# Gaps of 64 bytes between the x and y tiles of a two-layer encoder trunk

## The chip, the cores and the metric

The kernel runs on one core of a Trainium2 chip. The metric is device time in microseconds of one execution. TensorE (PE) multiplies: a LDWEIGHTS instruction (shown as engine PEld) puts a 128x128 stationary operand into the array, a MATMUL streams the moving operand through it; both operands are read from SBUF, and the load for one matmul runs while the matmul before it streams. DVE is VectorE, ACT is ScalarE, POOL is GpSimd, SP issues most DMAs.

## The reference

Two layers over 256 tokens of width 2048. Each is RMSNorm, a token mixer, a residual add, RMSNorm, a gated MLP with a convolution of width 3, a residual add; a last RMSNorm closes it.

```python
h = x
for layer in range(2):
    hn = rmsnorm(h, norm_mix_g[layer])
    h = h + (mlstm_mixer(hn, ...) if layer == 0 else hgrn_mixer(hn, ...))
    h = h + conv_glu(rmsnorm(h, norm_ffn_g[layer]), ffn_w_up[layer], ...)   # D_FF = 5504
return rmsnorm(h, final_g)
```

All is float32. By far the most work is the products of the activations with the weights (mixer in and out, MLP up and down).

## The kernel before

**Float32 in halves.** Every weight is split into a coarse part `wh` and a rest `wl` (lines 144 and 145, ACT and DVE), every activation tile into a coarse half and a rest that lie side by side in one tile of 512 columns (`split`, line 205: columns 0 to 255 are the coarse part of the 256 tokens, 256 to 511 the rest). A product is the sum of three, coarse by coarse, coarse by rest and rest by coarse, all in the float32r form.

**The stream of weights.** One list of chunks runs through the whole kernel (`stream`, line 149). Raw weights come by DMA into three buffers `raw` of 8192 bytes in each partition; pieces of 1024 columns are split into one of four buffers `wh` and one of four `wl` (4096 bytes each). Each chunk loops over k, the 128-row blocks of the contraction, with the activation tile `x = ch.x(k)`. Two forms of chunk do nearly all the work:

- "fm" (features by tokens; the mixers' q, k and gate inputs and MLP up; lines 197 to 200): for each of two column blocks f of the weights, the weights are stationary and the x tile moves: a matmul of 512 columns with `wh`, then one of 256 columns (the coarse half) with `wl`. So two loads and 768 moving columns make one pair.
- "tm" (tokens by features; v, o, gates, the mixers' outputs and MLP down; lines 187 to 191): a quarter of the x tile (128 columns) is stationary, 512 columns of the weights move; three matmuls of 512 columns for each half of the tokens. The last piece of the last chunk has the same three at lines 176 to 178.

A small first chunk has both forms (lines 189 to 194). Side jobs (mixer heads, transposes, norms) are put between these matmuls by a counter of estimated time (`Side.tick`).

**Where the tiles lie.** A pool puts the tiles of its tags one behind the other, in the order in which a tag is first used, each rounded up to 32 bytes; the pools follow one another. The x tiles (`xt0` to `xt15`, line 232) and y tiles (tags `yt0` to `yt15`, `slot`, line 378) are 2048 bytes each and lie in the pool `keep`, with one buffer each. y tiles hold the mixer's output (`ya`, `yb`) or the MLP's inner activations (`g`). The MLP's inner width is worked in two parts of 22 and 21 blocks; blocks 16 to 21 don't find a place among the sixteen y tiles and lie in the pool `ff` instead (line 379: `where = keep if j < KT else more`). In the built program the byte addresses in a partition are:

| tile | address | modulo 512 |
|---|---|---|
| hx (the residual stream) | 25664 | 64 |
| xt0 ... xt15 | 42048 ... 72768, steps of 2048 | 64 |
| ya0/g0/yb0 ... ya15/g15/yb15 | 74816 ... 105536, steps of 2048 | 64 |
| raw, three | 107584, 115776, 123968 | 64 |
| wh, four | 132160 ... 144448, steps of 4096 | 64 |
| wl, four | 148544 ... 160832, steps of 4096 | 64 |
| g16 ... g21, MLP of layer 0 | 179584 ... 189824, steps of 2048 | 384 |
| g16 ... g21, MLP of layer 1 | 187840 ... 198080, steps of 2048 | 448 |

The slices that a matmul takes start at multiples of 512 bytes in their tiles. Here *distance* means the start of the moving operand less the start of the stationary one, modulo 512. It is 0 for every fm and tm matmul, but for the tm matmuls of MLP down with g16 to g21, where it is 192 in layer 0 (64 - 384) and 128 in layer 1 (64 - 448). Those are 6 or 5 blocks by 2 halves by 3 matmuls, 36 or 30 in each of 16 chunks, 528 in all.

Of the kernel before, what the change touches and what calls it, by code (L numbers as in the profile page):

```python
# [8 lines left out]
F32 = mybir.dt.float32  # L9
F32R = mybir.dt.float32r  # L10
# [5 lines left out]
P = 128  # L16
T = 256
D = 2048
KT = D // P
# [23 lines left out]
RAW = 3  # L43
WB = 4
MIX = 4
FIRST = (0, 1, 2, 4, 7, 10, 13, 16)

LEVELS = (1, 2, 4, 8, 16, 32, 64)
# [4 lines left out]
def trunk_kernel(ctx, tc, xT, x_d, fg_d, pp_d, cst_d, w_first, w_aq, w_ak, w_av, w_ao, w_aout,  # L53
# [4 lines left out]
    keep = ctx.enter_context(tc.tile_pool(name="keep", bufs=1))  # L58
# [9 lines left out]
    hmx = keep.tile([P, 2], F32, name="mhalf")  # L68
    hx = keep.tile([P, KT, T], F32, name="hx")
    hT = [hx[:, k] for k in range(KT)]  # L70
    hm = hx.rearrange("p k t -> p (k t)").rearrange("p (a c) -> p a c", a=2)
    ident = cst[:, C_ID:C_ID + P]

# [45 lines left out]
    def split_weights(chunks):  # L119

        first = True
        for ch in chunks:
            total = ch.nk * ch.width
            cuts = [0]
            if first:
                cuts = [k * ch.width for k in FIRST]
            while cuts[-1] < total:
# [469 lines left out]
    def hgrn(norm, nxt):  # L597
# [24 lines left out]
        def blocks(z, h, a, b):  # L622
            v = z[:, 0:2 * (T + h)].rearrange("k (p x) -> k p x", p=2)[:, :, a:b]
            return v.rearrange("k p (m j) -> k m p j", j=2 * h)[:, :, :, 0:h]
# [32 lines left out]
        def head(hd):  # L657
# [11 lines left out]
            def gather(z, h, tag):  # L669
                m = mp.tile([P, T], F32, tag=tag, bufs=MIX, name=tag)  # L670
                dve.tensor_copy(m.rearrange("k (m p j) -> k m p j", p=2, j=h), blocks(z, h, 0, T))  # L671
                return m
# [229 lines left out]
def build(nc, ins, out_shape=(2, P, D), **kw):  # L902
    ap = {k: nc.dram_tensor("in_" + k, a.shape, mybir.dt.from_np(a.dtype), kind="ExternalInput").ap()
          for k, a in ins.items()}
    out = nc.dram_tensor("out", out_shape, F32, kind="ExternalOutput").ap()
    mscr = nc.dram_tensor("mscr", (64, T), F32, kind="Internal").ap()
    with tile.TileContext(nc, schedule_with_timeline_sim=True) as tc:
        with ExitStack() as ctx:
            trunk_kernel(ctx, tc, ap["xT"], ap["x"], ap["fg"], ap["pp"], ap["cst"], ap["w_first"],
                         ap["w_aq"], ap["w_ak"], ap["w_av"],  # L910
                         ap["w_ao"], ap["w_aout"], ap["w_bq"], ap["w_bv"], ap["w_bg"],
                         ap["w_bout"], ap["w_up"], ap["w_down"], out, mscr, **kw)
# [12 lines left out]
```

## Time and profile before

| | |
|---|---|
| time, median of 3 runs | 2473.65 us (2473.45 to 2473.66) |
| the profiled execution | 2473.85 us |
| its span (first to last instruction) | 2472.1 us |
| granted TensorE clock, mean | 0.999 |
| fm matmuls | 3776 of 512 columns (line 199), 3776 of 256 (line 200) |
| tm matmuls | 3 x 1442 (lines 189 to 191), 3 x 14 (lines 176 to 178) |

Matmuls are pipelined: a 512-column matmul is shown with a duration near 0.39 us though the next starts 0.23 us later. So the speed of PE is read from start to start, or from the number of instructions in a stretch, not from the durations; "busy" for PE means only that something was in flight. A line of the timeline has the start in us, the duration, the engine, the kernel's line and the operation, output<-inputs and their shapes. A line of the windows view has, for a stretch, its length, PE's busy time with the count of its instructions, the granted clock, and the DMA share and rate.

### The profile page before, as it was taken

To read this page: it belongs to the slowest core of one execution; us is meant where nothing else is said; L and a number is where in the kernel's file an instruction comes from. 1 tells how busy PE (TensorE), PEld (TensorE's weight loads), DVE (VectorE), ACT (ScalarE), POOL (GpSimd) and SP (SyncE) were. 2 spreads that over 40 slices of the span, in tenths; PEclk is the share of its full clock that TensorE was granted. 3 is DMA by queue.
4 is the path that set the end of the run, shared out by engine and by line. 5 is a ranking of instruction groups with operands and counts; after the bars stand their busy time and mean duration, and the time that the engine had idled before them with its cause. 6 is when DMAs were issued, how large, how long until landed. Compare 5 with 4: busy or idle time off the path is not lost.

```text
span 2472.1 us, 33659 instructions
## 1 busy us (share of the span) xinstructions
PE 2459.1 (99%) x13032; PEld 2102.3 (85%) x13032; DVE 1719.2 (70%) x2816; ACT 1188.3 (48%) x1751; POOL 153.4 (6%) x235
## 2 busy tenths in 40 slices
PE   9999999999999999999999999999999999999998
PEld 7888888888888888888888888888888888888887
DVE  7766656777645777657888888895677754677754
ACT  6555455454434444445444444445544543444443
POOL 0100000000000000002212222220000000000000
PEclk9999999999999999999999999999999999999999
DMA  7654555555555555555444444445555555655554
GB/s 287 198 175 170 179 176 188 188 189 190 192 190 193 188 188 187 171 187 186 163 156 168 154 165 157 156 154 205 187 188 188 190 185 189 203 186 185 186 186 143
DMA packets 66192, 452.06 MB, mean 183 GB/s; under 512 B 7648, under 2 KB 8032, under 8 KB 13424
## 3 DMA queue, kind: packets, MB, share of 16 engines
q1 hardware_dynamic: 63792, 443.29, 53.4%
q0 software_dynamic: 1232, 5.31, 0.8%
q8 instruction: 102, 1.67, 0.3%
q10 hardware_dynamic: 1008, 1.32, 0.1%
q14 instruction: 58, 0.48, 0.1%
HBM read 447.72 MB, written 2.16 MB: 182 GB/s over the span
## 4 chain that ended last, share of the span: by engine, by line
PE 93%; DVE 5%; issue 1%; ACT 1%; DMA 0%; SPq 0%; POOLq 0%; POOL 0%; DVEq 0%
PE mm L199 34%; PE mm L200 17%; PE mm L190 12%; PE mm L191 12%; PE mm L189 12%; DVE wl L145 2%; PE pd L688 2%; DVE QK L689 1%; PE pn L499 1%; DVE km L671 1%; PE py L713 1%; PE pz L268 0%; DVE AT L666 0%; DVE qm L671 0%; ACT wh L144 0%
## 5 line engine op out<-in xcount | busy, mean ns | idle before, releaser
L145 DVE TENSOR_TENSOR wl<-raw,wh 128x1024 fp32r<-128x1024 f32 (+1 forms) x848 | 1030.5, 1216 | 608.9 <-ACT wh L144 600.4
L199 PE MATMUL mm<-xt,wh 128*128 128x512 f32 x3776 | 1329.5, 397 | 0.0
L144 ACT CAST wh<-raw 128x1024 fp32r<-128x1024 f32 (+1 forms) x848 | 881.7, 1041 | 925.7 <-PE mm L191 441.5
L200 PE MATMUL mm<-xt,wl 128*128 128x256 f32 x3776 | 1056.5, 280 | 0.0
L199 PEld LDWEIGHTS mm<-xt,wh 128*128 128x128 f32 x3776 | 708.6, 188 | 166.0
L200 PEld LDWEIGHTS mm<-xt,wl 128*128 128x128 f32 x3776 | 711.8, 188 | 1.2
L191 PE MATMUL mm<-wh,g 128*128 128x512 f32 x674 | 263.9, 392 | 0.0
L189 PE MATMUL mm<-wh,g 128*128 128x512 f32 x674 | 263.6, 391 | 0.0
L190 PE MATMUL mm<-wl,g 128*128 128x512 f32 x674 | 263.4, 391 | 0.0
L189 PE MATMUL mm<-wh,xt 128*128 128x512 f32 x512 | 203.6, 401 | 1.8 <-ACT xt L206 1.8
L190 PE MATMUL mm<-wl,xt 128*128 128x512 f32 x512 | 204.4, 399 | 0.4 <-DVE wl L145 0.4
L191 PE MATMUL mm<-wh,xt 128*128 128x512 f32 x512 | 202.6, 397 | 0.0
L211 ACT COPY b<-mm 128x256 f32<-128x256 f32 x237 | 87.9, 371 | 183.6 <-PE mm L200 183.6
L191 PEld LDWEIGHTS mm<-wh,g 128*128 128x128 f32 x674 | 126.6, 188 | 27.5
L190 PEld LDWEIGHTS mm<-wl,g 128*128 128x128 f32 x674 | 126.6, 188 | 27.2
L189 PEld LDWEIGHTS mm<-wh,g 128*128 128x128 f32 x674 | 126.6, 188 | 27.2
L189 PEld LDWEIGHTS mm<-wh,xt 128*128 128x128 f32 x512 | 96.1, 189 | 20.3 <-ACT xt L206 2.1
L190 PEld LDWEIGHTS mm<-wl,xt 128*128 128x128 f32 x512 | 97.0, 189 | 18.5 <-DVE wl L145 0.8
L191 PEld LDWEIGHTS mm<-wh,xt 128*128 128x128 f32 x512 | 97.0, 189 | 18.0
L212 DVE TENSOR_TENSOR a<-mm,b 128x256 f32<-128x256 f32 x86 | 36.5, 425 | 54.8 <-ACT b L211 54.8
L688 PEld LDWEIGHTS pd<-qm,km 128*128 128x128 f32 x448 | 62.9, 191 | 10.2 <-PE mm L191 4.2
L688 PE MATMUL pd<-qm,km 128*128 128x128 f32 x448 | 66.1, 276 | 1.2 <-DVE qm L671 1.1
(200 smaller groups left out, 1933.9 us busy)
## 6 DMA issues: line engine op xcount, KB each, us to landing
raw<-in_w_up SPq DMA_DIRECT2D x172, 1024.0 KB, 5.0
raw<-in_w_down SPq DMA_DIRECT2D x80, 1024.0 KB, 4.8
raw<-in_w_bq SPq DMA_DIRECT2D x48, 1024.0 KB, 5.0
raw<-in_w_ao SPq DMA_DIRECT2D x16, 1024.0 KB, 4.9
raw<-in_w_aout SPq DMA_DIRECT2D x16, 1024.0 KB, 4.8
raw<-in_w_bv SPq DMA_DIRECT2D x16, 1024.0 KB, 5.0
raw<-in_w_bg SPq DMA_DIRECT2D x16, 1024.0 KB, 4.8
raw<-in_w_bout SPq DMA_DIRECT2D x16, 1024.0 KB, 4.9
```

The costliest lines, as they stand in the source:

```text
L144: act.copy(wh[:, :m], r)
L145: dve.tensor_tensor(wl[:, :m], r, wh[:, :m].bitcast(F32), ALU.subtract)
L189: pe.matmul(ps[t], xh, wh[:, c], start=st, stop=False)
L190: pe.matmul(ps[t], xh, wl[:, c], start=False, stop=False)
L191: pe.matmul(ps[t], xl, wh[:, c], start=False, stop=sp)
L199: pe.matmul(ps[f], wh[:, c:c + P], x, start=st, stop=False)
L200: pe.matmul(ps[f][:, 0:T], wl[:, c:c + P], x[:, 0:T], start=False, stop=sp)
L211: act.copy(b, ps[:, T:2 * T])
L212: dve.tensor_tensor(dst, ps[:, 0:T], b, ALU.add)
L499: pe.matmul(pn[:, 0:258], w, v, start=(i == 0), stop=(i == len(parts) - 1))
L671: dve.tensor_copy(m.rearrange("k (m p j) -> k m p j", p=2, j=h), blocks(z, h, 0, T))
L688: pe.matmul(pd[:, c], km[:, c], qm[:, c], start=True, stop=True)
```

## The change

`keep` gets 18 small tiles that nothing writes or reads: one of 16 floats (64 bytes) behind `hx`, one ahead of xt2, xt4, ..., xt14 and of yt2, ..., yt14, one behind xt15 and one behind yt15. To fix the order, the x and y tags are used once, ahead of their first real use, in a loop over all 32; these first tiles are never written.

```diff
@@ -43,6 +43,7 @@
+LEAD = 16
@@ -68,6 +69,14 @@
     hT = [hx[:, k] for k in range(KT)]
+    keep.tile([P, LEAD], F32, name="lead")
+    for j in range(2 * KT):
+        kind, i = ("xt", j) if j < KT else ("yt", j - KT)
+        if i % 2 == 0 and i:
+            keep.tile([P, 16], F32, name=f"gap{j}")
+        keep.tile([P, 2 * T], F32R, tag=f"{kind}{i}", name=f"{kind}{i}")
+        if i == KT - 1:
+            keep.tile([P, 16], F32, name=f"rest{j}")
```

By this text everything behind `hx` moves by 64 bytes, couple c of x (tiles 2c and 2c+1) by 64c more, the y tiles by 512 + 64c more, and all behind them (`raw`, `wh`, `wl`, the rest) by 64 + 16 x 64 = 1088 bytes, which is 64 modulo 512. So the start of an x or y tile less that of a weights' tile is 64c modulo 512 with c from 0 to 7: the distance in the sense above is 64c for fm matmuls and 512 - 64c for tm matmuls. For g16 to g21 it stays 192 and 128. No instruction is added or taken away.

## The prediction

> **What bounds the kernel.** I read the page's busy shares and chain first, then which engine is ever waited for, then the rate of the matmuls by stage and by operand address.
>
> ```profile
> span 2472.1 us, 33659 instructions
> ...
> PE 2459.1 (99%) x13032; PEld 2102.3 (85%) x13032; DVE 1719.2 (70%) x2816; ACT 1188.3 (48%) x1751; POOL 153.4 (6%) x235
> ...
> PE 93%; DVE 5%; issue 1%; ACT 1%; DMA 0%; SPq 0%; POOLq 0%; POOL 0%; DVEq 0%
> ```
>
> PE is in flight for all but 13 us and holds 93% of the chain of waits; the waits that end at PE come to under 5 us in all. So a nanosecond more or less from one matmul's start to the next is a nanosecond of the kernel, nearly everywhere. The change adds no instruction, so all it can do is alter that rate through the addresses. Whether addresses matter at all can be read from the trace, because one place already has another distance: MLP down, where block 16 is the first in the pool `ff`. Here the timeline of PE passes from g15 to g16 in layer 0:
>
> ```profile
> 666.93 0.39 PE L189 MATMUL mm<-wh,g 128*128 128x512 f32 x1
> 667.16 0.39 PE L190 MATMUL mm<-wl,g 128*128 128x512 f32 x1
> 667.39 0.39 PE L191 MATMUL mm<-wh,g 128*128 128x512 f32 x1
> ...
> 668.29 0.40 PE L189 MATMUL mm<-wh,g 128*128 128x512 f32 x1
> 668.53 0.39 PE L190 MATMUL mm<-wl,g 128*128 128x512 f32 x1
> 668.76 0.40 PE L191 MATMUL mm<-wh,g 128*128 128x512 f32 x1
> 668.99 0.39 PE L189 MATMUL mm<-wh,g 128*128 128x512 f32 x1
> 669.23 0.40 PE L190 MATMUL mm<-wl,g 128*128 128x512 f32 x1
> 669.46 0.39 PE L191 MATMUL mm<-wh,g 128*128 128x512 f32 x1
> 669.69 0.40 PE L189 MATMUL mm<-wh,g 128*128 128x512 f32 x1
> ```
>
> From 666.93 to 668.29 are six matmuls, 1.36 us, 226.7 ns each, at distance 0. From 668.29 to 669.69 are six more of the same form, 1.40 us, 233.3 ns each, at distance 192. Nothing else differs. Taking start times of all such stretches: distance 0 undisturbed 226 to 227 ns; the 144 and 120 matmuls at distance 192 (layer 0) 233.3; those at 128 (layer 1) 232.5 to 233. All 16 chunks show it. So address does set the rate, and distance 0, which the kernel has nearly everywhere, is the better of the three distances that tm matmuls show.
>
> The fm form has distance 0 throughout, yet two rates. The windows view, up-projection of layer 0, first and second part:
>
> ```profile
> 440.00:640.00 200.00, 200.00 (x1156) 1.00 0.58 190
> 780.00:1000.00 220.00, 220.00 (x1248) 1.00 0.57 187
> ```
>
> 200 us hold 1156 matmuls and 220 us 1248, so a pair (512 + 256 columns) takes 346 and 353 ns; from the start times 346.7 and 353.3. Each rate holds for a whole run of chunks, at the same clock (1.00) and addresses; both layers have the fast one in the first part and the slow one in the second. So the interplay of load and stream also has a phase that persists. Over all 3776 pairs the mean is 350.6 ns. The steps, 6.6 ns in each case, are alike: I read them as one more unit of stall for one load (tm: one load a matmul) or every second load (fm: two loads a pair).
>
> **The change, part by part.**
>
> *The tiles that nothing uses, and the early first use of the tags.* No instruction, no DMA, no queue is passed. 1088 bytes more are needed; the highest tile before ends at 225984, so all stays placed. The relative addresses of the tiles in the later pools do not change. Cost 0; if a first, never written tile made its successor wait, that wait would fall in the first few us, under 2 us.
>
> *tm matmuls.* 3 x 1442 + 3 x 14 = 4368, less the 528 at g16 to g21, which keep their distance: 3840 at distance 0 now. Couple 0 keeps it; 7/8, that is 3360, get distances 448, 384, ..., 64. Price: couples 5 and 6 land on exactly the measured 192 and 128: 233.3 - 226.7 = 6.6 ns more. For 384, 320 and 256 there is no row; bounds are 0 (as at distance 0) and 6.6; I take 6.6, since both distances measured away from 0 have it. For 448 and 64, the neighbours of 0, I look at the mixer head's products, whose distances lie from 448 to 504:
>
> ```profile
> 90.33 0.29 PE L499 MATMUL pn<-Vh,Wh 128*128 128x258 f32 x1
> ...
> 92.49 0.40 PE L190 MATMUL mm<-wl,xt 128*128 128x512 f32 x1
> ```
>
> 18 matmuls of 258 columns in 2.16 us, 120 ns each, against 116.7 ns for the mean 256-column one of line 200: hardly more. So half of 6.6 for these two couples. Sum: 5/8 of 3840 = 2400 by 6.6 is 15.8 us, 960 by 3.3 is 3.2 us, 19 us together. Against it: not all of the 3840 run at 226.7 now; in the mixers, where side jobs break in, they take 228 to 230 (all 3840: about 1 ns above the floor), which is 3360 by 1 ns, 3.4 us. **+16 us** (bounds 0 and 22).
>
> *fm pairs.* 7/8 of 3776, 3304 pairs, get distances 64 to 448; no fm row shows any. Bound above by the price per load: the better state plus two units, 346.7 + 13.2 = 360 ns, 9.4 over today's mean, 31 us. Bound by form: a 512-column matmul away from 0 takes 233.3 (tm rows), a short one 120 less 0.8 for its two columns (head rows), 352.5 to 353.5, which is the slower state that the fm form already has: about +3 ns, 10 us. Bound below: all pairs fall into the better state, -3.9 ns, -13 us. I take 4.5 ns, nearer to the state that this form does show: **+15 us**.
>
> *Cover.* In the second mixer (1126 to 1680 us) VectorE is busy 474 of 554 us and PE has some 17 us of gaps above its normal rate, where it waits for `wl` and the head's operands. About a fifth of both terms, 6 us, falls there, and a slower PE eats part of those gaps: **-2 us**. Elsewhere, past the start, the gaps come to under 6 us, so nothing hides the rest. DMA and the splitting of weights have slack (ACT 48%) and only wait longer for free buffers.
>
> Sum: 16 + 15 - 2 = +29 us on 2473.85, which is **2503 us** (+1.2%). The profiled execution lies 0.2 us above the median of the runs, and 1.75 above its span; both stay.
>
> **What the skill says.** The Trainium skill, TensorE: Matmul & The Clock Gate, Part 2, Step-by-step, holds that the array's stationary and moving operands have separate read ports: "Loading the next tile's weights doesn't steal SBUF read bandwidth from the running matmul." By that no distance could matter and the change would come out at 2474. The trace differs: 226.7 against 233.3 ns for one form at two distances. The same page's section Back-to-back issue gap gives N/2.4 + 2.5 ns, 215.7 at 512 columns; if that held at some distance, 11 ns a matmul would be there to win; no 512-column row here goes below 225.
>
> **Rivals.**
>
> 1. *Faster: varied distances break the persistent bad phase.* Place: the fm pairs at 353.3 (second part of both MLPs, most of the first mixer, some of the second). For it: the state holds for 240 us on end, so it is a lock, and a distance that jumps every fourth pair can't hold one. Against: jumps disturb the good lock too; where side jobs break in, tm runs at 228 to 230 rather than 226.7. It decides if the neutral distances outnumber the bad. All pairs at 346.7: 3776 by 3.9 is -15 us, 2459. If also the distances that no row shows (64, 256, 320, 384) were 5 ns better a load than today, half of 11,400 loads win: -28 more, 2430.
> 2. *No effect*: the rate follows the phase alone and 192 and 128 are chance; or the skill's rule. Against: 16 chunks of 16, within 1 ns. 2470 to 2478.
> 3. *Much slower*: the stream, once it meets the load at the same place, stays behind it to the load's end; far distances then cost several units instead of one. At three units more on half of the loads (5700 by 20 ns): +114 us, 2588. Against: 192 and 128 cost one unit each, and the head's products at 448 to 504 none.
> 4. *The gaps are not placed as the text says* (rounded away or put elsewhere): 2474. Tiles of 8 and 32 bytes already lie 32 apart, so 64 bytes hold.
>
> **Chances.** Forecast (slower, 2480 to 2535): 0.60. Rival 3: 0.10. Rivals 2 and 4: 0.07. Rival 1: 0.23. A measurement of this kernel can tell 0.2%, 5 us. So faster 0.23, same 0.07, slower 0.70. The likeliest case's own range is 2485 to 2530; for 8 in 10 I take in most of rival 1 (to 2450) and the upper bounds of both terms with some of rival 3 (2473.85 + 22 + 31 = 2527, to 2540).
>
> **What would show it.** Right: six tm matmuls in 1.36 us only for tiles 0 and 1 of a chunk and in about 1.40 for tiles 4 to 13; fm pairs between 350 and 360, changing every four pairs, no more 240 us of one rate. Instruction counts as before. Wrong: any couple below 226 ns, or fm pairs under 346, would make rival 1; rates as before within a chunk, rival 2.

## The result, and the profile after

2486.82 us (median of 4 runs, 2486.64 to 2487.22) against 2473.65 us before: +13.2 us, a ratio of 1.0053 with a 95% interval of 1.0036 to 1.0071. Slower, as forecast, by less than half of the forecast +29 us, and inside the range of 2450 to 2540. The span of the profiled execution is 2485.4 us.

The page of the changed kernel, busy shares and chain:

```profile
span 2485.4 us, 33659 instructions
...
PE 2471.8 (99%) x13032; PEld 2107.6 (85%) x13032; DVE 1719.6 (69%) x2816; ACT 1187.9 (48%) x1751; POOL 153.4 (6%) x235
...
PE 98%; DVE 1%; ACT 0%; issue 0%; DMA 0%; SPq 0%; POOLq 0%; POOL 0%; DVEq 0%
```

The same instructions, PE in flight for 12.7 us more, VectorE, ScalarE and GpSimd as busy as before to within 0.5 us: the time is in the rate of the matmuls. The chain of work that ended last now lies in PE for 98% rather than 93%.

Where the rate changed is seen in the first chunk of MLP down in layer 0. The lines are the first matmuls with g0, g2, g4, ... and g16 in PE's timeline (start, duration; line 198 is line 189 of before):

```profile
652.47 0.39 PE L198 MATMUL mm<-wh,g 128*128 128x512 f32 x1
...
655.22 0.40 PE L198 MATMUL mm<-wh,g 128*128 128x512 f32 x1
...
658.02 0.39 PE L198 MATMUL mm<-wh,g 128*128 128x512 f32 x1
...
660.81 0.39 PE L198 MATMUL mm<-wh,g 128*128 128x512 f32 x1
...
663.56 0.39 PE L198 MATMUL mm<-wh,g 128*128 128x512 f32 x1
...
666.29 0.40 PE L198 MATMUL mm<-wh,g 128*128 128x512 f32 x1
...
669.09 0.39 PE L198 MATMUL mm<-wh,g 128*128 128x512 f32 x1
...
671.88 0.39 PE L198 MATMUL mm<-wh,g 128*128 128x512 f32 x1
...
674.64 0.39 PE L198 MATMUL mm<-wh,g 128*128 128x512 f32 x1
```

Twelve matmuls lie between two of these lines. The eight couples take 2.75, 2.80, 2.79, 2.75, 2.73, 2.80, 2.79 and 2.76 us; at the old 226.7 ns each would take 2.72. The couples 0 to 3 (distances 0, 448, 384, 320) and 4 to 7 (256, 192, 128, 64) repeat the same four numbers to within 0.02 us. So the rate has a period of 256 bytes, not 512: 256 costs next to nothing, and 320 costs as little as 64. Over the whole trace the mean time to the next start by distance, without the matmuls that a side job breaks into, is

```
distance           0     64    128    192    256    320    384    448
tm, ns         228.0  229.6  232.5  233.1  228.1  229.9  232.1  233.0
fm pair, ns    350.7  351.5  349.1  351.9  350.9  351.5  348.9  352.0
```

For fm the same period holds, but all four values lie within 2 ns of the 350.6 ns that the two rates before averaged. The windows view shows what became of the two rates, first and second part of layer 0's up-projection:

```profile
440.00:640.00 200.00, 200.00 (x1142) 1.00 0.57 186
780.00:1000.00 220.00, 220.00 (x1256) 1.00 0.57 189
```

The first stretch held 1156 matmuls before and holds 1142 now (350 ns a pair instead of 346), the second held 1248 and holds 1256 (350 instead of 353). With the jumps, the good rate is gone as well as the bad one. By stage this is +2.8 us for each first part and -1.7 us for each second part.

Put together from the start times of the two traces, which have the same matmuls in the same order: tm chunks +10.3 us, the first chunk +0.2, fm chunks +3.0, all else -0.1: +13.4 from first to last matmul.

The start times also show what lies behind these means. In MLP down of the kernel before, an undisturbed tm matmul at distance 0 takes 226 or 227 ns every time. At 192 the times alternate between 236 and 231 ns, there and in the changed kernel, and at 64 (couple 3 of the changed one) they go round 232, 226 and 229. A distance thus sets a repeating pattern, and its rate is the mean of the pattern.

### The profile page after: what moved, and what is told of

Same layout as the page of the kernel before. It is cut to its first block, busy times and chain, and to the rows that moved or that the text cites. A ratio compares the mean times of both kernels' runs of the same rounds, so it can differ in the third digit from the quotient of the medians.

```text
span 2485.4 us, 33659 instructions
## 1 busy us (share of the span) xinstructions
PE 2471.8 (99%) x13032; PEld 2107.6 (85%) x13032; DVE 1719.6 (69%) x2816; ACT 1187.9 (48%) x1751; POOL 153.4 (6%) x235
## 4 chain that ended last, share of the span: by engine, by line
PE 98%; DVE 1%; ACT 0%; issue 0%; DMA 0%; SPq 0%; POOLq 0%; POOL 0%; DVEq 0%
PE mm L208 35%; PE mm L209 18%; PE mm L200 13%; PE mm L199 13%; PE mm L198 13%; PE pd L697 2%; PE pn L508 1%; PE py L722 1%; PE pz L277 0%; DVE wl L154 0%; PE S L494 0%; DMA raw<-in_w_first 0%; PE pd L687 0%; DVE QK L698 0%; PE pd L709 0%
```

## The experiments

Theories: D, a matmul's rate follows from its own distance modulo 256; M, the period is 512; S, it is the jumps from couple to couple that cost, not a distance; P, the rate of an fm chunk hangs on how it is entered. All edits below are to the kernel before. A loop that uses the x and y tags once, as in the change, fixes the order of the tiles where needed.

**One uniform distance.** Only one unused tile behind the last y tile, of 256, 128 or 64 bytes:

```diff
     hT = [hx[:, k] for k in range(KT)]
+    for j in range(2 * KT):
+        kind, i = ("xt", j) if j < KT else ("yt", j - KT)
+        keep.tile([P, 2 * T], F32R, tag=f"{kind}{i}", name=f"{kind}{i}")
+    keep.tile([P, 64], F32, name="rest")      # 256 bytes; 32: 128 bytes; 16: 64 bytes
```

> The kernel before with one unused tile of 256 bytes behind the last y tile, so that every distance that was 0 is 256 and none changes from block to block. Theory D (the rate goes by the distance alone, and with a period of 256 bytes, since the changed kernel's matmuls at d and d + 256 take the same time): tm matmuls 227 to 228 ns, fm pairs near 350.6 ns, 2470 to 2477 us. Theory M (the period is 512, and 256 is far from the good 0): tm at 233 ns, 3840 x 6 ns, 2490 to 2500 us. Theory S (it is the jumps of the distance every two blocks that cost, not a distance): 2470 to 2477 us, as D.

Measured 2473.73 us, ratio 0.9998 (0.9989 to 1.0007). By stage no difference from before exceeds 0.3 us; fm has the same two rates in the same places. M falls, and the unused tile and the early use of the tags cost nothing that this measurement can tell.

> The same with 128 bytes: all distances that were 0 are 384 for fm and 128 for tm, without jumps. Theory D: tm 232.5 ns, 3840 x 5.0 ns = +19 us; fm 349 ns as in the changed kernel at 384, 3776 x -1.6 = -6 us; together 2487 us (2483 to 2494). Theory S: no jumps, so no loss, 2473 us (2470 to 2477).

Measured 2492.39 us, ratio 1.0076 (1.0063 to 1.0089). S falls: without any jump the kernel is slower than the changed one. tm 232.4 ns as D has it. It is the difference of the addresses that counts and not either one: here the weights stand at 192 and the activations at 64 (modulo 256), in the kernel before the weights stood at 64 and g16 of layer 1 at 192, with 232.4 ns too. The fm term was wrong: the 349 ns that this distance had among jumps is not its steady rate, which is 350.9 to 351.1 in every stage of the MLPs. That the time still fell into D's range is in part luck: fm came out 10 us above its term, and tm 4 us below.

> The same with 64 bytes: distance 448 for fm, 64 for tm. Theory D: tm 229.6 ns, 3840 x 2.1 = +8 us; fm 352 ns as in the changed kernel at 448, 3776 x 1.4 = +5 us; together 2487 us (2481 to 2492). Theory S: 2473 us (2470 to 2477).

Measured 2491.51 us, ratio 1.0071 (1.0057 to 1.0085). tm 229.5 on average, as expected; fm steady at 353.2 and in both parts alike. The windows view of this run:

```profile
440.00:640.00 200.00, 200.00 (x1134) 1.00 0.57 185
780.00:1000.00 220.00, 220.00 (x1247) 1.00 0.57 186
```

200 us hold 1134 matmuls, 220 us 1247: 353 ns a pair in both, where distance 0 had 346 and 353. So the slow rate needs no jumps and can fill both parts. But tm, too, can have two rates at one distance. The first chunk of MLP down in layer 0 and the second have the same distance of 64; lines that are twelve matmuls apart, two in each chunk (line 193 is line 189 of before), are

```profile
659.82 0.39 PE L193 MATMUL mm<-wh,g 128*128 128x512 f32 x1
...
662.57 0.39 PE L193 MATMUL mm<-wh,g 128*128 128x512 f32 x1
...
690.33 0.40 PE L193 MATMUL mm<-wh,g 128*128 128x512 f32 x1
...
693.13 0.40 PE L193 MATMUL mm<-wh,g 128*128 128x512 f32 x1
```

Twelve matmuls take 2.75 us in the first chunk (229 ns each) and 2.80 in the second (233.3), from its start to g15. The third chunk is like the first and the fourth like the second; in all other stages the chunks take 229 to 230. A distance therefore fixes which rates there are, and not always one.

**The jumps alone.** Gaps of 256 bytes between the couples of x:

```diff
+    for i in range(KT):
+        if i % 2 == 0 and i:
+            keep.tile([P, 64], F32, name=f"gap{i}")
+        keep.tile([P, 2 * T], F32R, tag=f"xt{i}", name=f"xt{i}")
+    keep.tile([P, 64], F32, name="rest")
```

> Gaps of 256 bytes between the couples of x (2048 bytes in all), y not spread: from couple to couple the distance of x to the weights jumps by 256, between 0 and 256. Theory D with the period of 256 that the run with all distances at 256 bears out: no matmul changes, 2473.7 us (2472 to 2476), fm pairs in the same two rates 346.7 and 353.3. Theory S (the jumps themselves break the phase): the two rates of fm give way to a mean near 350.6 within a chunk, and tm with xt rises to 228 to 230 ns; 2474 to 2480 us.

Measured 2473.64 us, ratio 1.0000 (0.9991 to 1.0008), both fm rates in their places. Jumps by a whole period do nothing.

**The y tiles alone.** The change's loop, with the first tile of 64 bytes behind `hx`, but with gaps (and the last one) for y only:

> The change for the y tiles alone; x stays at distance 0 to the weights, so fm matmuls keep 0. In the trace of the changed kernel the tm matmuls with ya, yb and g took 8.0 us more than before, those with xt, the fm matmuls and the first chunk 5.4 us. Theory D, terms that add up: 2473.65 + 8.0 = 2481.7 us (2480 to 2484), with the two rates of the fm pairs, 346.7 and 353.3, back. Theory P (the phase in which an fm chunk is entered depends on the tm chunk ahead of it, so that y's distances shift the fm rates too): fm pairs in another mixture of the two rates, 2468 to 2494 us.

Measured 2477.40 us, ratio 1.0016 (1.0007 to 1.0025); below D's range. The tm matmuls with ya, yb and g cost 8.2 us more (8.0 expected), but one fm stage fell from the slow to the fast rate though its own distances stayed 0: the second part in layer 0, -4.5 us.

```profile
440.00:640.00 200.00, 200.00 (x1156) 1.00 0.58 190
780.00:1000.00 220.00, 220.00 (x1271) 1.00 0.58 191
```

1271 matmuls in 220 us (346 ns a pair) instead of 1248. So the fm rate of a stage does not follow from its own distance alone, as P has it, and the one that is caught is kept for 240 us. That what ran ahead decides is the likeliest reading and is not shown: this run also moves all that lies behind `hx` by 64 bytes, which no run tried alone, and the second part in layer 1 kept its slow rate behind the same distances of g0 to g15.

**The last six blocks at distance 0.**

```diff
             box["mp"] = stack.enter_context(tc.tile_pool(name="ff", bufs=1))
+            box["mp"].tile([P, 32 if layer else 48], F32, name="shift")
```

> The kernel before with an unused tile of 192 bytes (layer 0) or 128 bytes (layer 1) at the front of the pool of the MLP, so that g16 to g21 too have distance 0 to the weights. Theory D: their 528 matmuls fall from 233 to 226.7 ns, -3.3 us, 2470.4 us (2469 to 2472), with the fm rates unchanged. Theory P (the rate of an fm chunk hangs on the phase in which the tm chunk ahead leaves it): the second parts of the MLPs, which follow those matmuls, change their fm rate too; if both go from 353.3 to 346.7, 1370 pairs x -6.6 ns = -9 us more, 2461 us; if they stay, 2470.4 us.

Measured 2470.03 us, ratio 0.9986 (0.9977 to 0.9995), as D has it (-3.7 us in the trace). The timeline at the place where the kernel before went from 1.36 to 1.40 us for six:

```profile
668.34 0.39 PE L189 MATMUL mm<-wh,g 128*128 128x512 f32 x1
...
669.02 0.39 PE L189 MATMUL mm<-wh,g 128*128 128x512 f32 x1
...
669.70 0.39 PE L189 MATMUL mm<-wh,g 128*128 128x512 f32 x1
```

g16 starts at 668.34 and six matmuls take 1.36 us. The fm rates did not move, so the distance of the matmuls just ahead is not by itself what picks between the two.

**Steps below 64 bytes.** The uniform edit with 32 and with 224 bytes:

> One unused tile of 32 bytes behind the last y tile: distance 480 (224 by the period of 256) for fm, 32 for tm. By the steady rates so far, tm 226.7 at 0, 229.6 at 64, and fm 353.2 at 192, 346.7 or 353.3 at 0. Theory D, linear between neighbours: tm 228.1, 3528 x 1.4 = +5 us from the stages without the start; fm one rate between 350 and 353, +1 to +9 us; 2480 to 2488 us. Rival (below 64 bytes the distance does not count, as a line is fetched whole): 2473.7 us.

Measured 2500.50 us, ratio 1.0108 (1.0095 to 1.0122). Both forecasts miss: tm at 32 is 233.3, worse than at 64, so the cost isn't linear in the distance, and 32 bytes count. fm at 480 (224) has two rates, with a mean of 352.4: the mixers have chunks of either, and all four up-projections keep the slow one.

```profile
440.00:640.00 200.00, 200.00 (x1135) 1.00 0.57 189
780.00:1000.00 220.00, 220.00 (x1247) 1.00 0.57 187
```

200 us hold 1135 matmuls and 220 us 1247: 352 to 353 ns a pair in both.

> One unused tile of 224 bytes behind the last y tile: distance 288 (32 by the period) for fm, 224 for tm. Theory D, linear between neighbours: tm 230 ns between 233.2 at 192 and 226.7 at 0, 3528 x 3.3 = +12 us; fm at 32 between 0 (346.7 or 353.3) and 64 (351.5 in the changed kernel, no steady row), 347 to 352, -11 to +5 us; 2475 to 2491 us. Rival (below 64 bytes the distance does not count, rounded down): tm as at 192, fm as at 0, 2473.7 + 20 = 2494 us.

Measured 2480.22 us, ratio 1.0026 (1.0016 to 1.0036). tm at 224 is 233.2 (the tm chunks take 18.4 us more in the trace), and fm at 288 (32) gains 11.6 us: the up-projections take the fast rate in both parts, and chunks with side jobs among them take at most 348. The time lies in D's range because two misses offset each other: tm was to cost 12 us, and fm to gain 11 at the most.

```profile
440.00:640.00 200.00, 200.00 (x1156) 1.00 0.58 191
780.00:1000.00 220.00, 220.00 (x1271) 1.00 0.58 189
```

So the best distance for tm, 0, and one at which fm showed the fast rate alone, 32, are different.

**All steps of 16 bytes, and the two best together.** The buffers of the split weights get 256 bytes more, and each piece an offset `o` in them:

```diff
-                    wh = wpool.tile([P, 1024], F32R, tag="wh", bufs=WB, name="wh")
-                    wl = wpool.tile([P, 1024], F32R, tag="wl", bufs=WB, name="wl")
+                    o = 56 if ch.kind == "fm" else 0      # survey: 4 * (n_ % 16), chunk n_
+                    wh = wpool.tile([P, 1024 + 64], F32R, tag="wh", bufs=WB, name="wh")[:, o:o + 1024]
+                    wl = wpool.tile([P, 1024 + 64], F32R, tag="wl", bufs=WB, name="wl")[:, o:o + 1024]
```

> Buffers wh and wl 256 bytes wider; the pieces of chunk n are put 16 x (n mod 16) bytes into them (the first chunk at 0), so that chunks run through all distances in steps of 16 bytes, fm at minus that, tm at plus that. Theory D: each chunk settles at a rate of its distance: tm 226.7 at 0, 233.2 at 32, 229.6 at 64, 232.4 at 128, 233.2 at 192 and 224; fm 346.8 at 32, 353.2 at 192, 351.1 at 128, a mean near 352 at 224; the rest of the steps unknown, between 340 and 361 for a pair. Theory P: chunks of one distance scatter as much as chunks of different ones. Time 2473 to 2500 us.

One run, 2487.91 us. Each distance has 5 to 9 fm chunks and 1 to 5 tm chunks. Chunks of one distance agree within 1 ns for most distances and differ between distances, as D has it; the medians of the chunks, from the start times (in brackets a second rate that some chunks of that distance took), are

```
distance mod 256    0     16     32     48     64     80     96    112
tm, ns          226.6* 231.6  233.3  233.3  229.1  231.0  233.3  231.1
fm pair, ns     346.6  353.2  346.6  350.0  353.2  353.4  350.0  349.2
  second rate  (353.4)(346.6)              (348.8)(349.2)
distance mod 256  128    144    160    176    192    208    224    240
tm, ns          232.4  233.3  234.1  232.9  233.3  234.6  233.0  226.9*
fm pair, ns     350.8  353.2  346.6  353.2  353.2  346.5  346.6  346.8
* where no side job breaks in; with side jobs 228 to 233
```

No distance has a rate below 226.6 ns for tm or 346.5 for a pair: the fast rates of the kernel before are about the floor of these sixteen. One rate in this table doesn't mean that a distance has only one: at 224 all fm chunks here are fast, and in the run with 32 bytes whole stages at 224 took 353.3.

> Buffers wh and wl 256 bytes wider; pieces of fm chunks are put 224 bytes into them, pieces of tm and first chunks at 0, and g16 to g21 are shifted to distance 0 as before: fm distance 32, tm distance 0 everywhere. Theory D: every fm pair at 346.8 ns, as with all distances at 224, which took 11.6 us off the fm matmuls in that run's trace; tm at 226.7 also for g16 to g21, -3.7 us; 2473.7 - 15.3 = 2458.4 us (2456 to 2462). Theory P (fm's rate hangs on how the chunk is entered and not on its own distance): the two rates remain, 2470 us.

With the shift of g16 to g21 from above. Measured 2458.76 us, ratio 0.9939 (0.9926 to 0.9953): 15 us faster than the kernel before, 28 faster than the changed one, and D's 2458.4. In the trace fm has -11.9 us, and the windows show the fast rate in both parts:

```profile
440.00:640.00 200.00, 200.00 (x1156) 1.00 0.58 191
780.00:1000.00 220.00, 220.00 (x1268) 1.00 0.58 191
```

## Why the prediction was wrong in size

- *PE bounds, and only the rate from start to start can change.* Right: the 13.4 us between the two traces lie in tm, fm and first-chunk matmuls, and the runs at 256 bytes show that tiles of this kind cost nothing.
- *Distances 192 and 128 cost tm 6.6 ns.* Nearly right: at 192 it is 233.0 to 233.4 in every run that has it, at 128 232.0 to 232.8, so 128 costs 5.7 ns. The reading as one unit of stall for every load does not hold: at 192 the times alternate between 236 and 231 ns.
- *tm, +16 us: mis-sized.* Measured +10.5 with the first chunk. The step that failed is "For 384, 320 and 256 there is no row; ... I take 6.6, since both distances measured away from 0 have it." With a period of 256, distance 256 is distance 0 and 320 is 64 at 2.1 ns; 448 in turn is 192, and costs 5.5 ns where I took 3.3. The mean over the eight is 3.3 ns above the 227.5 of before; my sum had 5.0, less 0.9 for matmuls off the floor. For 3840 matmuls 3.3 ns are 12.6 us; most of the 2 us that are missing lie at the 152 matmuls that a side job follows, which took 1.1 us less than before and not more.
- *fm, +15 us: mis-sized.* Measured +3.0. The step is "I take 4.5 ns". It set the price against the mean of the two rates and left room up to 360 ns for loads that are all stalled; no distance has that (the worst median in the tables is 353.4). Each steady rate lies between 346.5 and 353.4, and among jumps the means are 349 to 352, about the mean of the old two, so what the first parts lost (2 x 2.8 us) the second parts gave back in good part (2 x 1.7).
- *Cover, -2 us.* About half: in the second mixer tm and fm rows account for 2.3 us (765 by 2.0 ns, 694 pairs by 1.1), and the stage became 1.2 us longer, so 1.1 us were hidden.
- *Rivals.* The first had its mechanism right and its balance wrong: the persistent bad phase was broken, together with the good one. The second is refuted: one unused tile of 128 bytes makes the kernel 18.7 us slower. So the rule of the Trainium skill (TensorE: Matmul & The Clock Gate, Part 2, Step-by-step) by which a weight load doesn't take read bandwidth from the running matmul does not give the time here; that it is read bandwidth that is lost was not shown either. The third is refuted by the table: no distance costs tm more than 8 ns or an fm pair more than 7.

What stays open: what picks between two rates at one distance was not settled. The run with y alone changed it, the run with g16 to g21 moved did not. What in the chip stands behind the period of 256 bytes was not shown. Nor was it told apart whether a matmul's own stationary operand counts or the next one, whose load runs meanwhile: both have the same distance except where one couple meets the next.

## What to carry to other kernels

Where PE streams back to back and loads new weights for every matmul, compare the start-to-start times of one form at different addresses before touching the order of the work: here the offset between the two operands, modulo 256 bytes, is worth up to 3.5% of a matmul (226.6 to 234.6 ns). Spreading the offsets over all values averages good and bad; setting each form to its own best offset (0 for one, 32 bytes for the other, by a slightly wider buffer) gained 15 us. Where a distance has two rates, look for one that shows only the fast one, and in a run where whole stages have it: a few chunks at 224 bytes looked safe here and were not.

## What the runs showed of the hardware that was not expected

- The rate depends on the distance between moving and stationary operand with a period of 256 bytes, and 16 or 32 bytes count: tm takes 226.7 ns at 0, 231.6 at 16, 233.3 at 32, 229.1 at 64. The rate is the mean of a repeating pattern: 236 and 231 ns in turn at 192.
- A distance that is good for one form need not be good for the other: 32 is the floor for fm (346.6) and near the worst for tm (233.3); 64 is good for tm (229.1) and among the worst for fm (353.2).
- At distance 0 an fm pair has two rates, 346.7 and 353.3 ns, each stable for a whole run of chunks (240 us) at the same granted clock and the same addresses; at 32 only the fast one was seen, in the undisturbed chunks of three runs. tm has two rates at 64, 229 and 233.3 ns, in neighbouring chunks of one stage.
